# A macaron transformer block on one core: two mixer low parts made by accumulating transfers, a new order of the first matmuls of two norms, and the last sums, squares and output scalings in another order

## The chip, the cores and the metric

The kernel runs on one core of a Trainium2 chip. The metric is the device time of one execution in microseconds (us), median over the runs, lower is better. Before the change it is 996.78 us, the median of three runs (996.49, 996.78 and 1000.95).

TensorE multiplies, VectorE (DVE) and ScalarE (ACT) do the elementwise work, GpSimd (POOL) does a little of it and issues some transfers, and SyncE (SP) issues the others. Each engine works through its own instructions in their order and waits on semaphores for the others.

## The reference

One block over 512 tokens of width 1024, in float32. A vector `mod` of nine parts (shift, scale and gate for three sub-layers) comes from the condition `c`.

```python
u = modulate(rmsnorm(h, g_norm_ffn1[l]), sh1, sc1)
h = h + 0.5 * gt1 * swiglu(u, w_ffn1_in[l], w_ffn1_out[l])
u = modulate(rmsnorm(h, g_norm_mix[l]), sh2, sc2)
h = h + gt2 * token_mixing(u, ...)
u = modulate(rmsnorm(h, g_norm_ffn2[l]), sh3, sc3)
h = h + 0.5 * gt3 * swiglu(u, w_ffn2_in[l], w_ffn2_out[l])
...
return rmsnorm(h, g_final)
```

`swiglu` has 2816 hidden units. `token_mixing` projects `u` to pooling inputs, queries, keys, values and gates, and merges a pooling branch with a dilated attention.

## The kernel before, in words

**Layout.** Features lie on the partitions. `H[0..7]` hold h, 128 features by 512 tokens each. Most work near the norms is done in two halves of the tokens: A (called T1 in the output code) is tokens 0 to 255, B (T2) tokens 256 to 511.

**Precision.** Every product is made of three matmuls in a reduced 32-bit format: high part of the weight by high part of the activation, high by low, low by high (`mm3`, lines 363 to 365; the same three in `product` at 871 to 873 and in `plain` at 931 to 933). So each weight chunk of 128x1024 that a transfer brings to a `raw` buffer is split before use. `split_hi` has ACT copy it into the ring `whi` (L318), and `split_lo` has DVE subtract that from it into the ring `wlo` (L332). For chunks listed in `self.outer` the low part is made otherwise: ACT writes minus the high part into `wlo` (L314), and a transfer on POOL's queue adds the chunk from HBM onto it (L316), so that DVE has no part in it. Both rings have room for seven chunks. `fetch` issues the loads of the chunks on SP's queue (L241) when one of the three `raw` buffers comes free.

**The first feed-forward layer's last output part** runs in `out_quad` (seven products, i = 0 to 6, with sums of blocks, so that partial results are buffered in `kept`) and, for the last product, in `out_last`. There `to_h` adds a result to H (L877 from the buffers for H 4 to 7, L937 from a bank), `square` makes the squares for the next norm (ACT, L940), `add` sums them (DVE, L962), `stats_t` sums over the features by matmuls with ones (PE, L454), then ACT takes the root (L456), DVE the reciprocal (L459), and `spread` puts the result on all partitions by four matmuls (L464). `last(m)` is the end of one feature tile's second half. `more` splits weights ahead of need.

**The norm and the next layer's first matmuls.** `norm_steps` gives for each of eight feature tiles k three steps: DVE `ut` (L471), ACT the high part UH (L483), DVE the low part UL (L497). `head` (called for the mixer, n = 1, and for the second feed-forward layer, n = 2) starts the next layer while the norm is still being made: in half A for k = 0 to 3 the first three weight tiles (banks 0, 1, 2), then the fourth for the same k, then stats of half B, then k = 4 to 7 for all four, with the spread of half B between. The mixer's first four chunks are called base to base+3 here; base+3 is the fourth tile's.

**The end** (`out_last` with n = 2, then `out_end`). `scaled` multiplies H by the final gain into the output tile O (ACT, L944). Half A: ACT copies the spread norm into R (L572), POOL multiplies O 0 to 3 by it (`final_first`, L564), DVE multiplies O 4 to 7 by the bank itself (`final_second`, L564), SP stores. Half B: stats, root, reciprocal, spread (warm-up matmuls, L596, between), then the products of DVE and POOL and the stores.

**What sets the order.** Everything is written out by hand: the order of the calls in these functions is the order on every engine.

## Time and profile before

| | us |
|---|---|
| median of three runs | 996.78 |
| the profiled execution | 997.2 |
| its span, first to last instruction | 995.4 |
| TensorE busy, whole span | 980.2 |
| TensorE idle, 0 to 10 | 3.36 |
| TensorE idle, 10 to 320 | 0.27 |
| TensorE idle, 349 to 358 (head of the mixer) | 1.94 |
| TensorE idle, 400 to 480 | 0.47 |
| TensorE idle, 656.5 to 664 (head of the second feed-forward layer) | 0.14 |
| TensorE idle, 982.5 to 995.4 (the end) | 9.07 |
| VectorE / ScalarE / GpSimd busy | 828.1 / 565.1 / 70.8 |

The profiled execution was 0.4 us above the median. A row of the timeline gives start, length, engine, line, operation, tiles, count, and in brackets how long the engine was idle before it and whom it waited for. Lengths of neighbours overlap a little, so the cost of one among others is the distance of the starts.

### The profile page before, as it was taken

To read this page: it belongs to the slowest core of one execution; us is meant where nothing else is said; L and a number is where in the kernel's file an instruction comes from. 1 tells how busy PE (TensorE), PEld (TensorE's weight loads), DVE (VectorE), ACT (ScalarE), POOL (GpSimd) and SP (SyncE) were. 2 spreads that over 40 slices of the span, in tenths; PEclk is the share of its full clock that TensorE was granted. 3 is DMA by queue.
4 is the path that set the end of the run, shared out by engine and by line. 5 is a ranking of instruction groups with operands and counts; after the bars stand their busy time and mean duration, and the time that the engine had idled before them with its cause. 6 is when DMAs were issued, how large, how long until landed. Compare 5 with 4: busy or idle time off the path is not lost.

```text
span 995.4 us, 17274 instructions
## 1 busy us (share of the span) xinstructions
PE 980.2 (98%) x6962; PEld 916.0 (92%) x6962; DVE 828.1 (83%) x1260; ACT 565.1 (57%) x867; POOL 70.8 (7%) x80
## 2 busy tenths in 40 slices
PE   8999999999999999999999999999999999999996
PEld 6888899999999999889988888898999999999996
DVE  6979989999998877879667777578998989989875
ACT  6453286776768653233414323465677868676774
POOL 0000010110111000007100000000010110010001
PEclk9999999999999999999999999999999999999998
DMA  9867576877858422123364774223375566567522
GB/s 340 278 210 255 191 186 195 231 180 220 239 141 188 146 85 98 53 97 111 110 227 170 274 248 140 99 86 106 116 196 167 139 172 179 157 151 209 150 43 85
DMA packets 49746, 165.92 MB, mean 167 GB/s; under 512 B 5633, under 2 KB 8961, under 8 KB 49666
## 3 DMA queue, kind: packets, MB, share of 16 engines
q1 hardware_dynamic: 41778, 137.95, 39.5%
q0 software_dynamic: 7200, 26.22, 15.5%
q8 instruction: 54, 0.88, 0.3%
q10 hardware_dynamic: 688, 0.66, 0.2%
q14 instruction: 26, 0.21, 0.1%
HBM read 162.03 MB, written 2.77 MB: 166 GB/s over the span
## 4 chain that ended last, share of the span: by engine, by line
PE 92%; DVE 6%; issue 1%; ACT 1%; DMA 0%; DVEq 0%; ACTq 0%
PE bank L364 11%; PE bank L363 11%; PE bank L365 11%; PE bank L750 10%; PE bank L751 10%; PE bank L752 10%; PE bank L871 6%; PE bank L872 6%; PE bank L873 6%; PE bank L1751 1%; PE bank L1753 1%; PE bank L1755 1%; PE bank L1342 1%; DVE wlo L332 1%; DVE qz L1267 1%
## 5 line engine op out<-in xcount | busy, mean ns | idle before, releaser
L332 DVE TENSOR_TENSOR wlo<-raw,whi 128x1024 fp32r<-128x1024 f32 (+6 forms) x126 | 138.1, 1106 | 46.4 <-ACT whi L318 46.2
L363 PE MATMUL bank<-UH,whi 128*128 128x512 f32 (+1 forms) x432 | 158.1, 366 | 0.0
L364 PE MATMUL bank<-UL,whi 128*128 128x512 f32 (+1 forms) x432 | 154.2, 357 | 2.1 <-DVE UL L497 1.9
L318 ACT ACTIVATE whi<-raw 128x1024 fp32r<-128x1024 f32 (+5 forms) x157 | 149.1, 963 | 10.3 <-DMA raw<-wf1o 4.2
L365 PE MATMUL bank<-UH,wlo 128*128 128x512 f32 (+1 forms) x432 | 153.9, 356 | 0.0
L750 PE MATMUL bank<-UH,whi 128*128 128x256 f32 x512 | 141.4, 276 | 0.0
L752 PE MATMUL bank<-UH,wlo 128*128 128x256 f32 x512 | 141.4, 276 | 0.0
L751 PE MATMUL bank<-UL,whi 128*128 128x256 f32 x512 | 141.4, 276 | 0.0
L750 PE MATMUL bank<-SH,whi 128*128 128x256 f32 x384 | 107.0, 279 | 0.0
L752 PE MATMUL bank<-SH,wlo 128*128 128x256 f32 x384 | 106.9, 278 | 0.0
L751 PE MATMUL bank<-SL,whi 128*128 128x256 f32 x384 | 106.8, 278 | 0.0
L318 ACT ACTIVATE whi<-X 128x1024 fp32r<-128x1024 f32 (+2 forms) x98 | 91.9, 952 | 14.8 <-DVE X L257 14.7
L751 PEld LDWEIGHTS bank<-UL,whi 128*128 128x128 f32 x512 | 96.2, 188 | 0.1
L750 PEld LDWEIGHTS bank<-UH,whi 128*128 128x128 f32 x512 | 96.1, 188 | 0.1
L752 PEld LDWEIGHTS bank<-UH,wlo 128*128 128x128 f32 x512 | 96.1, 188 | 0.0
L364 PEld LDWEIGHTS bank<-UL,whi 128*128 128x128 f32 x432 | 81.2, 188 | 14.0 <-DVE UL L497 2.7
L332 DVE TENSOR_TENSOR wlo<-X,whi 128x1024 fp32r<-128x1024 f32 (+2 forms) x79 | 82.4, 1058 | 12.7 <-ACT whi L318 12.6
L365 PEld LDWEIGHTS bank<-UH,wlo 128*128 128x128 f32 x432 | 81.1, 188 | 12.1
L363 PEld LDWEIGHTS bank<-UH,whi 128*128 128x128 f32 x432 | 81.2, 188 | 11.4 <-issue 0.5
L871 PE MATMUL bank<-HI,whi 128*128 128x256 f32 x288 | 79.9, 277 | 0.0
L872 PE MATMUL bank<-HK,whi 128*128 128x256 f32 x288 | 79.5, 276 | 0.0
L873 PE MATMUL bank<-HI,wlo 128*128 128x256 f32 x288 | 79.5, 276 | 0.0
(349 smaller groups left out, 2456.0 us busy)
## 6 DMA issues: line engine op xcount, KB each, us to landing
ada<-wada SPq DMA_DIRECT2D x47, 512.0 KB, 5.3
raw<-wmix SPq DMA_DIRECT2D x44, 512.0 KB, 3.8
raw<-wf1i SPq DMA_DIRECT2D x33, 512.0 KB, 6.0
raw<-wf2i SPq DMA_DIRECT2D x31, 512.0 KB, 4.4
AR<-wada SPq DMA_DIRECT2D x16, 512.0 KB, 3.8
wlo<-wf2i POOLq DMA_DIRECT2D x16, 512.0 KB, 5.5
raw<-wf1o SPq DMA_DIRECT2D x15, 512.0 KB, 4.9
X<-wf2i SPq DMA_DIRECT2D x13, 512.0 KB, 7.1
```

The lines of the kernel that those rows point to most:

```text
L318: self.nc.scalar.activation(self.hi[:, y], r[:, x], AF.Copy)
L332: self.nc.vector.tensor_tensor(self.lo[:, y], r[:, x], self.hi[:, y], op=OP.subtract)
L363: M(ps, hi, uh, start=start, stop=False)
L364: M(ps, hi, ul, start=False, stop=False)
L365: M(ps, lo, uh, start=False, stop=stop)
L750: M(o, hi, uh, start=start and p == 0 and k == 0, stop=False, skip_group_check=True)
L751: M(o, hi, ul, start=False, stop=False, skip_group_check=True)
L752: M(o, lo, uh, start=False, stop=k == 3, skip_group_check=True)
L871: M(o, hi, uh, start=start and m % 2 == 0 and k == 0, stop=False, skip_group_check=True)
L872: M(o, hi, ul, start=False, stop=False, skip_group_check=True)
L873: M(o, lo, uh, start=False, stop=k == 1, skip_group_check=True)
L1267: self.nc.vector.tensor_scalar(qz[:, (2 * i + h) * P:(2 * i + h + 1) * P], q[:, toks], self.hmask[:, h:h + 1], None, op0=OP.mult)
```

## The change

- Four lines of `out_quad`: in the last output part H 4 to 7 get their buffered sums behind the copies of product 4, and no longer behind product 5.
- `plan`: base+2 and base+3 join `self.outer`. Their low parts are made by ACT and a transfer on POOL's queue.
- `head`: in half A for k = 0 to 3 the matmuls of the tiles in hand are grouped: all that take UH first, then those that take UL.
- `out_last` and `out_end`: `more` is called earlier a second time, with a limit of seven chunks from the part's start. In the second layer the scalings of half B leave their places behind each square, `final_second` is called twice, for O 4 and 5 ahead of `last(1)` and for O 6 and 7 behind the last sum, and three scalings stand behind the root.

```diff
+        self.outer.update({i: self.order[i][1] for i in (base + 2, base + 3)})
...
-    def final_second(self, rA):
+    def final_second(self, rA, m):
...
-        for j in range(4, KT):
+        for j in (m, m + 1):
             self.final(nc.vector, j, A, rA)
-            if j % 2:
-                self.store(j - 1, j + 1, A, nc.sync)
+        self.store(m, m + 2, A, nc.sync)
...
-        self.stats_t(rB, Bh, parts)
+        self.stats_t(rB, Bh, parts, between)
         warm(2)
-        nc.scalar.activation(self.O[3][:, Bh], self.H[3][:, Bh], AF.Copy, scale=self.g(3)[:, 3:4])
...
+                if h == 0 and i < 4:
+                    for x, y in ((0, 0), (1, 0), (0, 1)):
+                        for j in which:
+                            self.nc.tensor.matmul(banks[j][:, hs], w[j][k][x], (self.UH, self.UL)[y][k][:, hs],
+                                                  start=k == x == y == 0, stop=False)
+                    continue
...
                     copy(D[b][:, :, 1, :], r(A[b]))
-                elif i == 5 and tail:
-                    for m in (2 * b, 2 * b + 1):
+                    for m in (2 * b, 2 * b + 1) if tail else ():
                         to_h(4 + m, D[b][:, m % 2, :, :].rearrange("p h t -> p (h t)"), slice(0, T))
...
         def more():
-            if self.done < self.pos + 4:
+            if self.done < self.tail[n // 2] + 7:
...
-            if m < 3:
-                scaled(m, T2)
...
         pair(C, 0, T1, self.acc)
+        more()
         for m in (2, 3):
             plain(C, m, T1)
+        self.split_lo()
+        self.fetch()
...
-        if step:
+        if n:
+            self.final_second(rA, 4)
+            scaled(4, T2)
+            scaled(5, T2)
+        else:
             step(0)
-        for i in (4, 5, 6, 7):
-            scaled(i, T2)
-        more()
         last(1)
...
         sums.append(one(1))
+        scaled(6, T2)
...
-        self.split_lo()
-        self.fetch()
-        if n:
-            self.final_second(rA)
         last(3)
...
-        if not n:
+        if n:
+            self.final_second(rA, 6)
+            scaled(0, T2)
+            scaled(3, T2)
+        else:
             add(x, s)
+        self.fetch()
...
-            self.out_end(gate, (*self.late, s))
+            self.out_end((*self.late, s), lambda: [scaled(m, T2) for m in (1, 7, 2)])
```

**DVE, from the end of the first feed-forward layer into the mixer's norm.** H_72 to H_79 are H 0 to 7, AR holds the sums of squares, `sl` squares, raw_67 is the buffer of base+3. Before:

```order
L471 SCALAR_TENSOR_TENSOR ut<-H_74,mod,bank_104 128x256
L497 SCALAR_TENSOR_TENSOR UL<-ut,mod,UH 128x256
L937 SCALAR_TENSOR_TENSOR H_73<-bank_100,mod,H_73 128x256
L962 TENSOR_TENSOR AR<-AR,sl 128x256 x2
L332 TENSOR_TENSOR wlo<-raw_67,whi 128x1024
L471 SCALAR_TENSOR_TENSOR ut<-H_75,mod,bank_104 128x256
L497 SCALAR_TENSOR_TENSOR UL<-ut,mod,UH 128x256
L937 SCALAR_TENSOR_TENSOR H_75<-bank_101,mod,H_75 128x256
```

The same place after the change:

```order
L472 SCALAR_TENSOR_TENSOR ut<-H_74,mod,bank_104 128x256
L498 SCALAR_TENSOR_TENSOR UL<-ut,mod,UH 128x256
L941 SCALAR_TENSOR_TENSOR H_73<-bank_100,mod,H_73 128x256
L966 TENSOR_TENSOR AR<-AR,sl 128x256 x2
L472 SCALAR_TENSOR_TENSOR ut<-H_75,mod,bank_104 128x256
L498 SCALAR_TENSOR_TENSOR UL<-ut,mod,UH 128x256
L941 SCALAR_TENSOR_TENSOR H_75<-bank_101,mod,H_75 128x256
```

The subtraction of base+3's low part is gone from between the sums of squares and the fourth `ut`; the other steps stand as they stood. The one of base+2, some 25 rows earlier, is gone too, and there the four additions into H 4 to 7 now stand ahead of base+1's subtraction and no longer behind it. On ACT the two copies for each of base+2 and base+3 stand together ahead of squares of half A.

**PE, the first rows of the mixer's head.** bank_98, bank_99 and bank_102 are the first three weight tiles. Before:

```order
L363 MATMUL bank_98<-UH,whi 128x256
L364 MATMUL bank_98<-UL,whi 128x256
L365 MATMUL bank_98<-UH,wlo 128x256
L363 MATMUL bank_99<-UH,whi 128x256
L364 MATMUL bank_99<-UL,whi 128x256
L365 MATMUL bank_99<-UH,wlo 128x256
L363 MATMUL bank_102<-UH,whi 128x256
L364 MATMUL bank_102<-UL,whi 128x256
L365 MATMUL bank_102<-UH,wlo 128x256
```

After:

```order
L643 MATMUL bank_98<-UH,whi 128x256
L643 MATMUL bank_99<-UH,whi 128x256
L643 MATMUL bank_102<-UH,whi 128x256
L643 MATMUL bank_98<-UH,wlo 128x256
L643 MATMUL bank_99<-UH,wlo 128x256
L643 MATMUL bank_102<-UH,wlo 128x256
L643 MATMUL bank_98<-UL,whi 128x256
L643 MATMUL bank_99<-UL,whi 128x256
L643 MATMUL bank_102<-UL,whi 128x256
```

The first matmul that takes UL was the second of nine and is now the seventh. The head of the second feed-forward layer changes likewise.

**DVE at the end of the program.** `u` holds the late sums of squares, bank_98 the spread norm of half A. Before:

```order
L937 SCALAR_TENSOR_TENSOR H_74<-bank_100,mod,H_74 128x256
L937 SCALAR_TENSOR_TENSOR H_73<-bank_103,mod,H_73 128x256
L962 TENSOR_TENSOR u_9435<-u_9435,sl 128x256 x2
L564 TENSOR_TENSOR out<-out,bank_98 128x256 x4
L937 SCALAR_TENSOR_TENSOR H_75<-bank_100,mod,H_75 128x256
L962 TENSOR_TENSOR u_9435<-u_9435,sl 128x256
L459 RECIPROCAL r_90<-r_90 128x2
```

After:

```order
L941 SCALAR_TENSOR_TENSOR H_74<-bank_100,mod,H_74 128x256
L565 TENSOR_TENSOR out<-out,bank_98 128x256 x2
L941 SCALAR_TENSOR_TENSOR H_73<-bank_103,mod,H_73 128x256
L966 TENSOR_TENSOR u_9437<-u_9437,sl 128x256 x2
L941 SCALAR_TENSOR_TENSOR H_75<-bank_100,mod,H_75 128x256
L966 TENSOR_TENSOR u_9437<-u_9437,sl 128x256
L565 TENSOR_TENSOR out<-out,bank_98 128x256 x2
L460 RECIPROCAL r_90<-r_90 128x2
```

Two of the four output products now stand ahead of H 1's addition, two behind the last sum of squares.

More of the change, by code (lines that the diff above doesn't have):

```diff
@@ L576, in final_first, with out_end @@
                 self.store(j - 1, j + 1, A, nc.sync)
-    def final_second(self, rA):
+    def final_second(self, rA, m):
         nc, A = self.nc, slice(0, HT)
-        for j in range(4, KT):
+        for j in (m, m + 1):
             self.final(nc.vector, j, A, rA)
-            if j % 2:
-                self.store(j - 1, j + 1, A, nc.sync)
-    def out_end(self, gate, parts):
+        self.store(m, m + 2, A, nc.sync)
+    def out_end(self, parts, between):
         nc = self.nc
@@ L901, in out_quad @@
                     copy(D[b][:, :, 1, :], r(A[b]))
-                elif i == 5 and tail:
-                    for m in (2 * b, 2 * b + 1):
+                    for m in (2 * b, 2 * b + 1) if tail else ():
                         to_h(4 + m, D[b][:, m % 2, :, :].rearrange("p h t -> p (h t)"), slice(0, T))
-                elif i == 5:
+                elif i == 5 and not tail:
                     v.tensor_tensor(D[b][:, :, 0, :], r(B[b]), D[b][:, :, 0, :], op=OP.add)
```

## The prediction

> **What bounds the kernel now.** The page gives busy time over the span:
>
> ```profile
> PE 980.2 (98%) x6962; PEld 916.0 (92%) x6962; DVE 828.1 (83%) x1260; ACT 565.1 (57%) x867; POOL 70.8 (7%) x80
> ```
>
> PE is the bound, so what counts is where its 15 us of idle time lie. I read the same by stretches next. Columns: the stretch, its length, then busy time and instruction count of PE, its weight loads, DVE, ACT and POOL, then the granted clock, the DMA share and GB/s.
>
> ```profile
> 349.00:358.00 9.00, 7.06 (x59) 6.67 (x58) 8.20 (x20) 5.14 (x11) 0.00 (x0) 1.00 0.28 97
> 656.50:664.00 7.50, 7.36 (x61) 6.96 (x60) 6.51 (x18) 6.39 (x14) 0.00 (x0) 1.00 0.17 63
> 760.00:976.00 216.00, 216.00 (x1898) 216.00 (x1897) 187.36 (x233) 157.44 (x222) 18.28 (x21) 1.00 0.58 150
> 982.50:995.40 12.90, 3.83 (x30) 3.26 (x28) 4.87 (x14) 2.58 (x8) 2.50 (x4) 0.73 0.49 163
> ```
>
> PE has no gap in the long stretches (216.00 of 216.00 us, 1898 matmuls, 0.114 each). Work removed from DVE or ACT there is worth nothing. The change's two places are where PE does wait: the mixer's head, where it is idle 1.94 us of 9.00 while DVE is busy 8.20, and the end. PE's own waits name whom it waits for:
>
> ```profile
> PE bank L364 <- DVE UL L497: 1.9, 2, 1.1
> PE bank L454 <- DVE u L962: 1.5, 1, 1.5
> ```
>
> The first row is the mixer's head (two waits for low parts of u), the second the last sum of squares. Together they are 3.4 us of 995, so no outcome of this change that fills them reaches 0.5% (5.0 us), which is about what a measurement of this kernel can tell from no change.
>
> **Sums into H sooner, and the squares of the first layer's output.** DVE's rows, ACT's two, PE's one:
>
> ```profile
> 334.19 2.74 DVE L877 SCALAR_TENSOR_TENSOR H<-kept,mod,H 128x512 f32<-128x512 f32 x4
> 336.84 1.22 DVE L332 TENSOR_TENSOR wlo<-raw,whi 128x1024 fp32r<-128x1024 f32 x1
> 341.71 1.49 DVE L962 TENSOR_TENSOR AR<-AR,sl 128x512 f32<-128x512 f32 x2
> 331.96 2.00 ACT L318 ACTIVATE whi<-raw 128x1024 fp32r<-128x1024 f32 x2
> 338.49 0.81 ACT L940 ACTIVATE AR<-H 128x256 f32<-128x256 f32 x2 [4.52 <-DVE H L937]
> 343.51 0.94 PE L454 MATMUL bank<-ones,AR 128*128 128x1 f32 x8
> ```
>
> Moving the four additions (2.74) forward and dropping base+2's subtraction lets DVE reach H 0 about two to three us sooner. But the last sum ends at 341.71 + 1.49 = 343.20, and PE reaches the matmuls that read it at 343.51 without a wait: PE's own work hides all of it, so its price is nothing. The freed time pays for what ACT gets: two more copies of 1.0 us each (two took 2.00) and base+3's high part moved here, three in all, two of them between the first and the later squares. ACT had idled 4.52 before the squares, so the three fit and the last sum should not come later than today. Were that cover gone, each us would cost one. Queued behind the new ACT copies are those squares, behind them DVE's sums, behind those PE's statistics. The POOL queue gets two issues and nothing of its own stands behind them until the pooling some 100 us later; on SP the buffers of base+2 and base+3 come free from ACT and no longer from DVE, so the loads of base+5 and base+6 start sooner and nothing waits for them.
>
> **Two low parts by transfers: the mixer's head.** DVE's rows, then PE's:
>
> ```profile
> 348.87 0.48 DVE L497 SCALAR_TENSOR_TENSOR UL<-ut,mod,UH 128x256 fp32r<-128x256 f32 x1
> 350.32 1.22 DVE L332 TENSOR_TENSOR wlo<-raw,whi 128x1024 fp32r<-128x1024 f32 x1
> 351.46 0.48 DVE L471 SCALAR_TENSOR_TENSOR ut<-H,mod,bank 128x256 f32<-128x256 f32 x1
> 351.85 0.48 DVE L497 SCALAR_TENSOR_TENSOR UL<-ut,mod,UH 128x256 fp32r<-128x256 f32 x1
> 354.01 0.48 DVE L497 SCALAR_TENSOR_TENSOR UL<-ut,mod,UH 128x256 fp32r<-128x256 f32 x1
> 357.43 0.16 DVE L459 RECIPROCAL r<-r 128x2 f32<-128x2 f32 x1
> 351.04 0.28 PE L363 MATMUL bank<-UH,whi 128*128 128x256 f32 x1
> 352.39 0.38 PE L364 MATMUL bank<-UL,whi 128*128 128x256 f32 x1 [1.08 <-DVE UL L497]
> 354.54 0.38 PE L364 MATMUL bank<-UL,whi 128*128 128x256 f32 x1 [0.86 <-DVE UL L497]
> 355.59 0.95 PE L454 MATMUL bank<-ones,AR 128*128 128x1 f32 x8
> 357.90 0.61 PE L464 MATMUL bank<-cst,r 128*128 128x128 f32 x4
> ```
>
> The subtraction at 350.32 (base+3) stands in DVE's way between the third and fourth `ut`: 351.46 - 350.32 = 1.14 us by start to start. Without it the low parts of k = 2 and 3 end at 351.19 and 353.35 in place of 352.33 and 354.49. DVE goes on back to back from there, so the reciprocal of half B ends at 357.59 - 1.14 = 356.45.
>
> PE, with the UH matmuls first at 0.114 each: k = 2 starts at 351.04 as before, its six UH matmuls last to 351.72, and UL is there. Three more to 352.06, six of k = 3 to 352.74, then it waits for UL until 353.40 (0.05 behind its end, as before). The remaining three take 0.4 (eight took 355.59 - 354.54 = 1.05), statistics start at 353.8, and from there to the spread it is 357.90 - 355.59 = 2.31, so PE is at the spread at 356.1. But the spread reads the reciprocal of 356.45, so it starts at 356.50: **1.40 us sooner**. Grouping UH alone adds about 0.1 of that, since the reciprocal decides. Bounds: 1.14, if the spread keeps its old distance to the reciprocal, and 1.8, if PE's arrival decided. I take 1.40, because the row of the reciprocal is what the spread has to wait for.
>
> The two transfers must be in time. Landing of all 50 transfers of this kind (the row of the line that issues them, us):
>
> ```profile
> DMA to landing us min/median/max: 5.0/5.6/9.4
> ```
>
> ACT has written minus base+2's high part one copy behind base+1's, at 331.96 + 2.0 = about 333.9, and base+3's behind the first two squares, by 338.49 + 0.81 + 1.0 = 340.3 at the latest. The head starts 18 matmuls before 351.04, at 349.0; PE reads base+2's low part from the sixth on, 349.6, and base+3's from 353.8. So 15.7 and 13.5 us are there for 9.4 at most.
>
> [...]
>
> After 358 PE has almost no gaps and DVE's further steps hang on PE's banks, so I carry the whole 1.40 to the end.
>
> **High parts first in the second feed-forward layer's head.** PE's first wait and its spread, and DVE's reciprocal:
>
> ```profile
> 657.01 0.38 PE L364 MATMUL bank<-UL,whi 128*128 128x256 f32 x1
> 663.21 0.71 PE L464 MATMUL bank<-cst,r 128*128 128x128 f32 x4
> 662.99 0.16 DVE L459 RECIPROCAL r<-r 128x2 f32<-128x2 f32 x1
> ```
>
> PE no longer stalls at 657.01, but the spread at 663.21 already starts 0.06 behind the reciprocal's end (663.15), and DVE's chain to it is not touched. What PE wins early it waits at the spread: 0, with 0.1 at most either way.
>
> **The end.** DVE's rows, then POOL's, PE's, ACT's two, and the lengths of the late sums:
>
> ```profile
> 981.13 0.48 DVE L937 SCALAR_TENSOR_TENSOR H<-bank,mod,H 128x256 f32<-128x256 f32 x1 [0.73 <-PE bank L933]
> 981.54 1.45 DVE L962 TENSOR_TENSOR u<-u,sl 128x256 f32<-128x256 f32 x2
> 982.91 1.40 DVE L564 TENSOR_TENSOR out<-out,bank 128x256 f32<-128x256 f32 x4
> 984.24 0.47 DVE L937 SCALAR_TENSOR_TENSOR H<-bank,mod,H 128x256 f32<-128x256 f32 x1
> 984.63 0.41 DVE L962 TENSOR_TENSOR u<-u,sl 128x256 f32<-128x256 f32 x1
> 986.92 0.17 DVE L459 RECIPROCAL r<-r 128x2 f32<-128x2 f32 x1 [1.89 <-ACT r L456]
> 980.39 3.19 POOL L564 TENSOR_TENSOR out<-out,AR 128x256 f32<-128x256 f32 x4 [24.99 <-ACT AR L572]
> 985.10 0.61 PE L454 MATMUL bank<-ones,u 128*128 128x1 f32 x4 [1.52 <-DVE u L962]
> 980.82 2.10 ACT L944 ACTIVATE out<-H,vecs 128x256 f32<-128x256 f32 x5
> 988.35 0.38 ACT L606 ACTIVATE AR<-bank 128x256 f32<-128x256 f32 x1 [1.06 <-DVE out L564]
> L962 DVE TENSOR_TENSOR u<-u,sl x4: 409/634/954, 979.3 to 984.6; 128x256 f32<-128x256 f32 x3, 128x512 f32<-128x512 f32 x1
> ```
>
> The four output products (1.40, 0.35 each) stand between the sums and H 3's addition, on the path to PE's wait of 1.52. In the change two of them (0.70) fit into DVE's wait of 0.73 for PE before 981.13, and two stand behind the last sum, where DVE idles 1.89. So H 3's addition starts at 982.91 in place of 984.24, 1.33 us sooner, and its square on ACT with it. The last sum then starts at 983.30, while POOL still runs its products (980.39 to 983.58). Of the late sums the one in the clear took 0.409 and the longest, at POOL's side, 0.954: beside POOL it may cost up to 0.54 more. POOL will start some 0.1 to 0.2 sooner, since ACT no longer has a scaling (0.42) ahead of R, so only 0.1 of the overlap is left. I take **1.2**; bounds 0.8 (the whole 0.54) and 1.5 (POOL's earlier start freeing the first sum too).
>
> [...]
>
> On ACT three scalings stand behind the root where one stood. Five took 2.10, so two more cost 0.84, and ACT idles 1.06 there for DVE's first product: hidden, 0.1 late at most.
>
> **Sum.** 1.40 + 0 + 1.2 = 2.6. The profiled execution took 997.2, 995.4 of span and 1.8 around it, and would take 994.6. It stands 0.4 above the median of 996.78, so I forecast 994.2.
>
> **Rivals.**
>
> *The mixer's gain is given back.* Behind the head some DVE stretch, or a chunk's load, becomes the last to end, and PE only waits elsewhere. For it: DVE is over 80% busy over the span. Against: PE has no gap in the long stretches, and the list of its waits names no transfer. The end alone then gives 996.78 - 1.2 = 995.6.
>
> *The end's gain is lost to POOL and ACT.* The last sum takes the whole 0.54 and R comes 0.2 late: 996.78 - 1.4 - 0.6 = 994.8. For it is the 0.954 row.
>
> *The second head's gain stays.* If the reciprocal were not what the spread waits for, 0.4 more: 993.8. The reciprocal's row speaks against it.
>
> *Slower: the accumulating transfers come late.* Place: base+2's low part, read from 349.6. Nothing is lost until it lands 15.7 us after ACT's copy at 333.9; each us beyond is PE idle. To undo the 2.6 it would have to land at 352.2, 18.3 us after, about twice the longest of the 50. Then the time is 997 and above.
>
> **How the numbers follow.** Forecast 0.68, mixer's gain given back 0.14, end lost 0.10, second head 0.04, slower 0.04. The range takes both gains at their upper bounds and 0.1 for the second head (3.4, so 993.4) and 0.4 for the spread of runs, hence 993.0, and above the first rival with the end at its lower bound 0.8 (996.0) and the same 0.4, 996.4. Faster by over 0.5% needs 991.8, more than all the waits in reach, 0.02; slower by over 0.5% only in a part of the last rival, 0.02; the rest, 0.96, is within 0.5%.
>
> **What would show it.** In the profile after: in the mixer's head one short wait for UL (about 0.6) at k = 3 and a new one at the spread for the reciprocal; the spread 1.4 sooner after the head's start. In the second head no wait for UL but one of about 0.4 at the spread. At the end PE's wait for the last sum down from 1.52 to about 0.3, and a last sum longer than 0.409. Statistics of half A in the first layer without a wait. I am wrong if PE waits at the mixer's head for `wlo`, if it waits at 343.5 for the sums, or if its stretches between 358 and 976 show new gaps.

## The result and the profile after

| | before | after |
|---|---|---|
| median of 22 runs each, us | 998.08 | 994.70 |
| lowest to highest, us | 996.49 to 1005.30 | 993.96 to 998.76 |
| the profiled execution, us | 997.20 | 995.64 |

The ratio of after to before is 0.9958, with a 95% interval of 0.9942 to 0.9973. The forecast was 994.2 from 996.78, a ratio of 0.9974: just outside that interval, on the small side. The time itself, 994.7, is 0.5 from the forecast, and the ratio stands for no change by the 0.5% bound, though its interval reaches past it.

The run times lie in groups. Of before's 22, 13 are between 996.5 and 998.4 (median 997.20) and 9 between 1000.9 and 1005.3; of after's, 16 are between 994.0 and 995.6 (median 994.48) and 6 between 997.0 and 998.8. The lower groups differ by 2.72 us, close to the forecast's 2.6. The rest of the ratio comes from the upper groups, and a later run shows where before's begin.

The page of after, its row of busy times: PE is busy 1.1 us more than before, DVE 2.2 us less.

```profile
PE 981.3 (99%) x6962; PEld 916.8 (92%) x6962; DVE 825.9 (83%) x1258; ACT 567.2 (57%) x869; POOL 72.4 (7%) x82
```

The same three places by stretches, columns as before (PE, its weight loads, DVE, ACT, POOL, granted clock, DMA share, GB/s):

```profile
349.00:358.00 9.00, 8.29 (x70) 7.89 (x69) 7.80 (x21) 5.32 (x10) 0.00 (x0) 1.00 0.14 38
656.50:664.00 7.50, 7.02 (x61) 6.81 (x60) 6.51 (x18) 5.94 (x14) 0.00 (x0) 1.00 0.11 45
982.50:993.80 11.30, 4.05 (x30) 3.37 (x28) 4.21 (x12) 3.05 (x8) 2.35 (x4) 0.66 0.55 186
```

In the mixer's head PE is idle 0.71 of 9.00 us where it was idle 1.94. The second head shows more idle time than before, 0.48 against 0.14. The list of PE's waits names them:

```profile
PE bank L465 <- DVE r L460: 0.7, 2, 0.5
PE bank L643 <- DVE UL L498: 0.5, 1, 0.5
PE bank L455 <- DVE u L966: 0.2, 1, 0.2
```

The two waits for UL (1.9) became one of 0.5, the wait at the end went from 1.5 to 0.2, and there is a new kind: 0.7 in two waits of the spread for the reciprocal, one in each head. No row names `wlo` or the sums in AR. PE's rows at the four places (start, length, engine, line, tiles, count, in brackets the idle time before and whom it waited for):

```profile
343.88 0.95 PE L455 MATMUL bank<-ones,AR 128*128 128x1 f32 x8
...
349.36 0.50 PE L643 MATMUL bank<-UH,whi 128*128 128x256 f32 x3
...
353.77 0.63 PE L643 MATMUL bank<-UL,whi 128*128 128x256 f32 x3 [0.51 <-DVE UL L498]
354.24 0.95 PE L455 MATMUL bank<-ones,AR 128*128 128x1 f32 x8
356.88 0.71 PE L465 MATMUL bank<-cst,r 128*128 128x128 f32 x4 [0.21 <-DVE r L460]
...
662.55 0.71 PE L465 MATMUL bank<-cst,r 128*128 128x128 f32 x4 [0.48 <-DVE r L460]
...
983.77 0.61 PE L455 MATMUL bank<-ones,u 128*128 128x1 f32 x4 [0.23 <-DVE u L966]
```

From half A's statistics to half B's spread of the mixer's norm are 356.88 - 343.88 = 13.00 us; before they were 357.90 - 343.51 = 14.39. DVE's rows beside them:

```profile
341.18 1.48 DVE L966 TENSOR_TENSOR AR<-AR,sl 128x512 f32<-128x512 f32 x2
...
350.69 0.47 DVE L472 SCALAR_TENSOR_TENSOR ut<-H,mod,bank 128x256 f32<-128x256 f32 x1
...
356.66 0.16 DVE L460 RECIPROCAL r<-r 128x2 f32<-128x2 f32 x1
...
980.28 0.74 DVE L565 TENSOR_TENSOR out<-out,bank 128x256 f32<-128x256 f32 x2
...
982.77 0.47 DVE L941 SCALAR_TENSOR_TENSOR H<-bank,mod,H 128x256 f32<-128x256 f32 x1
983.16 0.55 DVE L966 TENSOR_TENSOR u<-u,sl 128x256 f32<-128x256 f32 x1
983.64 0.74 DVE L565 TENSOR_TENSOR out<-out,bank 128x256 f32<-128x256 f32 x2
```

The sums of half A end at 342.66, 1.2 us ahead of PE (0.31 before). The `ut` at 350.69 now stands directly behind DVE's sums of squares, with no subtraction between. The reciprocal's end, 356.82, decides the spread. At the end two output products stand ahead of H 1's addition and two behind the last sum.

### The profile page after: what moved, and what is told of

The parts are those of the page before. It is cut to its first block, busy times and chain, and to the rows that moved or that the text cites. A ratio compares the mean times of both kernels' runs of the same rounds, so it can differ in the third digit from the quotient of the medians.

```text
span 993.8 us, 17278 instructions
## 1 busy us (share of the span) xinstructions
PE 981.3 (99%) x6962; PEld 916.8 (92%) x6962; DVE 825.9 (83%) x1258; ACT 567.2 (57%) x869; POOL 72.4 (7%) x82
## 4 chain that ended last, share of the span: by engine, by line
PE 92%; DVE 6%; issue 1%; ACT 1%; DMA 1%; SPq 0%; DVEq 0%; ACTq 0%
PE bank L364 10%; PE bank L756 10%; PE bank L366 10%; PE bank L365 10%; PE bank L755 10%; PE bank L757 10%; PE bank L877 6%; PE bank L876 6%; PE bank L878 6%; PE bank L1759 1%; PE bank L1763 1%; PE bank L1761 1%; PE bank L1350 1%; DVE wlo L333 1%; DVE qz L1275 1%
## 5 line engine op out<-in xcount | busy, mean ns | idle before, releaser
L333 DVE TENSOR_TENSOR wlo<-raw,whi 128x1024 fp32r<-128x1024 f32 (+6 forms) x124 | 135.6, 1103 | 44.5 <-ACT whi L319 44.3
L364 PE MATMUL bank<-UH,whi 128*128 128x512 f32 (+1 forms) x408 | 151.6, 372 | 0.0
L366 PE MATMUL bank<-UH,wlo 128*128 128x512 f32 (+1 forms) x408 | 147.5, 362 | 0.0
L365 PE MATMUL bank<-UL,whi 128*128 128x512 f32 (+1 forms) x408 | 147.3, 361 | 0.0
L756 PEld LDWEIGHTS bank<-UL,whi 128*128 128x128 f32 x512 | 96.2, 188 | 0.1
L755 PEld LDWEIGHTS bank<-UH,whi 128*128 128x128 f32 x512 | 96.1, 188 | 0.1
L757 PEld LDWEIGHTS bank<-UH,wlo 128*128 128x128 f32 x512 | 96.1, 188 | 0.0
L366 PEld LDWEIGHTS bank<-UH,wlo 128*128 128x128 f32 x408 | 76.8, 188 | 12.1
L365 PEld LDWEIGHTS bank<-UL,whi 128*128 128x128 f32 x408 | 76.7, 188 | 11.4 <-issue 0.5
L364 PEld LDWEIGHTS bank<-UH,whi 128*128 128x128 f32 x408 | 76.7, 188 | 11.3 <-issue 0.5
```

Source lines behind the costliest of these rows:

```text
L333: self.nc.vector.tensor_tensor(self.lo[:, y], r[:, x], self.hi[:, y], op=OP.subtract)
L364: M(ps, hi, uh, start=start, stop=False)
L365: M(ps, hi, ul, start=False, stop=False)
L366: M(ps, lo, uh, start=False, stop=stop)
L755: M(o, hi, uh, start=start and p == 0 and k == 0, stop=False, skip_group_check=True)
L756: M(o, hi, ul, start=False, stop=False, skip_group_check=True)
```

## The experiments

The theory of the prediction: the mixer's head is quicker because transfers take base+3's subtraction off DVE, and the end because H 3's addition comes sooner. Its rival: the transfers have no part in it, and the subtraction only had to go elsewhere. Since the run times lie in groups, I compare the stages inside the traces, each from one landmark row of PE to another. "Head" is half A's statistics to half B's spread; "to second head" is the mixer's spread of half A to the same spread of the next norm; "second layer" goes from there to the same spread at the end; "end" is half A's statistics there to half B's first row that reads `u`. The ends of matmuls in these rows are modelled, and a bracket shows only the idle time behind such an end, so a wait of 0.1 or 0.2 us shows in the distance of two starts alone.

| kernel | head | to second head | second layer | end | median us |
|---|---|---|---|---|---|
| before | 14.39 | 307.89 | 325.41 | 8.29 | 998.08 |
| after | 13.00 | 306.87 | 326.03 | 6.99 | 994.70 |
| e1, no transfers | 13.11 | 306.85 | 325.40 | 7.00 | 995.41 |
| e2, late split | 16.04 | 310.34 | 325.40 | 6.99 | 998.10 |
| e3, no high part first | 13.23 | 307.20 | 325.40 | 6.98 | 994.59 |
| e4, spread later | 13.98 | 306.24 | 324.70 | 6.98 | 993.35 |
| e5, early split only | 13.57 | 307.02 | 325.41 | 8.28 | 1000.21 |
| e6, sums late | 13.10 | 306.90 | 325.41 | 6.99 | 994.12 |
| e7, old end | 12.99 | 307.05 | 325.41 | 8.28 | 995.55 |
| e8, no transfers, spread and copy moved | 14.17 | 306.14 | 324.70 | 6.99 | 993.75 |
| e9, spread and copy moved | 14.06 | 306.10 | 324.70 | 7.00 | 993.10 |
| e10, before again | 16.90 | 311.31 | 325.41 | 8.27 | 1001.52 (one run) |
| e11, before again | 14.37 | 308.51 | 325.41 | 8.28 | 997.56 (one run) |
| e12, after again | 12.99 | 306.67 | 325.40 | 7.00 | 994.60 (one run) |

In e4, e8 and e9 half B's spread stands a step later, so their "head" isn't comparable.

**e1: without the transfers.** Base+2 and base+3 get their low parts on DVE again, at the early place.

```diff
-        self.outer.update({i: self.order[i][1] for i in (base + 2, base + 3)})
```

> The changed kernel, but base+2 and base+3 are split as before (ACT high part, DVE subtraction) and keep their new early place. Theory (the mixer's head gains because DVE is freed of two subtractions, which only the transfers can do): DVE has the 2 x 1.14 us again, now between 334 and 341 where it has under 2 us free; the last sum of half A comes about 0.6 to 1.0 late, PE waits that long at the statistics near 343.9, and about 0.7 of the head's 1.4 us is lost. Rival (moving base+3's split out of DVE's dense stretch is enough, the transfers are for nothing): no wait at the statistics, head from its start to its spread as short as in the changed kernel (7.5 us; before 8.9), time within 0.2 us of the changed kernel.

Measured: 995.41 us (994.25 to 998.00), ratio 0.9956 (0.9936 to 0.9976), by the run times the same as the full change. DVE's rows, then PE's:

```profile
332.98 2.35 DVE L332 TENSOR_TENSOR wlo<-raw,whi 128x1024 fp32r<-128x1024 f32 x2
...
337.55 1.23 DVE L332 TENSOR_TENSOR wlo<-raw,whi 128x1024 fp32r<-128x1024 f32 x1 [1.43 <-ACT whi L318]
...
341.65 1.48 DVE L965 TENSOR_TENSOR AR<-AR,sl 128x512 f32<-128x512 f32 x2
```

```profile
342.81 0.28 PE L936 MATMUL bank<-HX,wlo 128*128 128x256 f32 x1
343.18 1.05 PE L454 MATMUL bank<-ones,AR 128*128 128x1 f32 x8
...
353.18 0.62 PE L642 MATMUL bank<-UL,whi 128*128 128x256 f32 x3 [0.51 <-DVE UL L497]
...
356.29 0.71 PE L464 MATMUL bank<-cst,r 128*128 128x128 f32 x4 [0.18 <-DVE r L459]
```

Base+3's subtraction stands at 337.55, behind a wait of DVE for ACT of 1.43 us, and the sums end at 343.13. PE's last matmul ahead of the statistics starts at 342.81. In after the statistics follow 0.12 behind that matmul (343.76 and 343.88); here they follow 0.37 behind it, just behind the sums, so they are 0.25 late. The head is 13.11 us, and from that last matmul to the spread are 13.48 us, against 13.12 in after and 14.51 before. So most of it is the rival's: 1.03 of the 1.39 us come without the transfers, from splitting base+3 early and, for 0.1 to 0.2, from the grouping (e3). The transfers are worth the other 0.36, about half of what the theory gave them.

**e2: the transfers, but the second split at its late place.** The call of `more` goes back to its old place ahead of `last(1)`, with its old limit; base+3's part then is copied and sent there.

```diff
-        more()
         for m in (2, 3):
...
+        more()
         last(1)
```

> The changed kernel, but the second call that splits ahead stands in its old late place, so base+3's two copies on ACT and its transfer come between the high parts of u of the mixer's norm. Theory (the transfer needs the early place): ACT writes minus the high part near 349.5, the transfer lands some 5.6 us later near 355, while PE wants base+3's low part near 354; PE waits for wlo 1 to 2 us and for the third high part of u up to 1 us, and most of the head's 1.4 us is gone (head from start to spread 8.5 to 10 us against 7.5). Rival (the place does not matter): head 7.5 us, no wait for wlo.

Measured: 998.10 us (996.32 to 1000.92), ratio 0.9991 (0.9971 to 1.0010): the whole gain is gone. PE's row, and the transfer's issue to landing in the groups of its line:

```profile
357.17 0.58 PE L366 MATMUL bank<-UH,wlo 128*128 128x256 f32 x1 [2.04 <-DMA wlo<-wmix]
```

```profile
DMA to landing us min/median/max: 7.4/7.4/7.4
```

The transfer is issued at 349.7 and lands 7.4 us after, so PE stands 2.04 us. That explains two thirds of the 3.04 by which the head is longer (16.04 against 13.00). The rest lies behind the wait, where PE's starts are 0.213 apart until 360, for 0.114 otherwise; e10 comes back to it. DVE has no subtraction of base+3 here either, so a free DVE isn't enough: the low part has to be there when PE reads it.

**e3: without the high parts first**, the grouping in `head` taken out.

```diff
-                if h == 0 and i < 4:
...
-                    continue
```

> The changed kernel, but both heads take the matmuls of one tile together again (UH high, UL high, UH low), as before. Theory (the spread's reciprocal decides, so grouping is worth about 0.1 us in the mixer's head and nothing in the second layer's): mixer's head from start to spread 7.6 us, second head 6.7 us as in the changed kernel, waits for UL back at both and no wait at the second spread. Rival (grouping is worth its own waits): mixer's head about 8.2 us, second head 7.1 us.

Measured: 994.59 us (993.87 to 997.04), ratio 0.9955 (0.9938 to 0.9973). PE's rows:

```profile
353.67 0.39 PE L365 MATMUL bank<-UL,whi 128*128 128x256 f32 x1 [0.85 <-DVE UL L498]
354.71 0.95 PE L455 MATMUL bank<-ones,AR 128*128 128x1 f32 x8
...
357.01 0.61 PE L465 MATMUL bank<-cst,r 128*128 128x128 f32 x4
```

PE waits once, for 0.85, and comes to the spread when the reciprocal is there. The grouping is worth 13.23 - 13.00 = 0.23 in the mixer's head, and 0.13 at the matmul behind the spread (at 357.37 here and 357.34 in after), since the spread behind its wait took 0.10 longer (0.71 against 0.61). The run times can't tell so little. In the second head, statistics to spread are 12.09 here, 12.06 in after, 12.08 before: worth nothing, because the spread there starts 0.05 to 0.07 behind the reciprocal's end either way.

**e4: half B's spread one product step later**, in both heads, to see whether the new waits for the reciprocal cost anything.

```diff
-                    if i == 8:
+                    if i == 9:
                         self.spread(self.B[7], Bh)
-                    if i > 7:
-                        stepB(i - 8)
+                    if i > 8:
+                        stepB(i - 9)
```

> The changed kernel, but in both heads the spread of half B and the norm steps behind it stand one k later (12 matmuls more before it). Theory (PE's waits at the two spreads, 0.21 and 0.48 us, are waits for the reciprocal alone, and the grouped order's gain in the second head lies hidden there): both waits go, about 0.7 us less in all, 0.2 before the mixer's body and 0.5 before the second layer's. Rival (the norm of half B then comes late and PE waits for its UL or UH in half B): the same or up to 1 us slower.

Measured: 993.35 us (992.59 to 995.68), ratio 0.9942 (0.9918 to 0.9965). In the list of PE's waits, after's row of 0.7 for the reciprocal is gone; what is left of the three places is the wait for UL and the one at the end:

```profile
PE bank L643 <- DVE UL L498: 0.5, 1, 0.5
PE bank L455 <- DVE u L966: 0.2, 1, 0.2
```

The stretch to the second head is 306.24, and the second layer 324.70 against 325.40: 0.4 to 0.6 (against e12 and after) and 0.7 us less. So the waits did cost. Each gain is more than the wait it removed (0.21 and 0.48); where the rest comes from isn't shown. The run's interval overlaps after's.

**e5: the early split alone**, on the kernel before: no transfers, the sums into H where they were, the old end.

```diff
-            if self.done < self.pos + 4:
+            if self.done < self.tail[n // 2] + 7:
...
+        more()
         for m in (2, 3):
```

> The kernel before with one edit: base+3 is split at the early place of the changed kernel, by ACT and DVE, no transfers, sums into H at their old place, old orders elsewhere. Theory (the early place gives the head's gain, and the sooner sums are the cover that pays for it): DVE now has base+3's 1.14 us and a wait for its high part between the first H additions, half A's last sum of squares ends near 345.8 in place of 343.2, and PE waits 2 to 2.5 us at the statistics of half A; the head after it is 1.1 to 1.3 us shorter (statistics of half A to spread of half B, 14.4 before, near 13.2), net about 1 us slower. Rival (the sooner sums are worth nothing, as the prediction had it): no wait at the statistics, 1.2 us faster.

Measured: 1000.21 us (998.35 to 1002.66), ratio 1.0009 (0.9993 to 1.0026). DVE's rows, then PE's:

```profile
343.19 1.23 DVE L332 TENSOR_TENSOR wlo<-raw,whi 128x1024 fp32r<-128x1024 f32 x1 [1.44 <-ACT whi L318]
...
347.29 1.48 DVE L962 TENSOR_TENSOR AR<-AR,sl 128x512 f32<-128x512 f32 x2
```

```profile
348.82 1.05 PE L454 MATMUL bank<-ones,AR 128*128 128x1 f32 x8 [2.24 <-DVE AR L962]
```

Now the subtraction's wait for ACT is on the path, and PE stands 2.24 us for the sums. Without that wait PE would have been there at 346.58, so this execution is also 3.07 us late from earlier on (below). From 346.58 to the spread of the second head at 658.35 are 311.77 us, against 310.19 before (343.51 to 653.70): 1.6 us slower, though the head behind the wait is shorter. The lowest run is 1.5 above before's lowest of that set (996.88). So the early split has to be paid for ahead of 343 us. A part of the loss is PE's granted clock, 0.52 from 351 to 353 us, behind the wait (see e10).

**e6: the sums into H back behind product 5**, everything else as changed.

```diff
-                    for m in (2 * b, 2 * b + 1) if tail else ():
+                elif i == 5 and tail:
+                    for m in (2 * b, 2 * b + 1):
```

> The changed kernel, with the buffered sums into H 4 to 7 back behind product 5. Theory (the transfers free as much of DVE as the sooner sums do, either covers the other): half A's last sum ends near 343.3, PE waits 0 to 0.2 us at the statistics, time within 0.2 us of the changed kernel, statistics of half A to spread of half B 13.0 us as there. Rival (the sums on time are what the early split needs in any case): a wait of 1 us or more at the statistics.

Measured: 994.12 us (994.00 to 994.53), ratio 0.9957 (0.9940 to 0.9974). PE's row:

```profile
343.15 1.05 PE L455 MATMUL bank<-ones,AR 128*128 128x1 f32 x8
```

The matmul ahead of it starts at 342.91, so the statistics are 0.12 late. With the transfers the earlier sums are hardly needed; without the transfers (e1) they are what pays, but for 0.25. Either of the two is nearly enough, the change has both, and with neither (e5) PE waits 2.24.

**e7: the old end**, everything else as changed.

```diff
-        if n:
-            self.final_second(rA, 4)
-            scaled(4, T2)
-            scaled(5, T2)
...
+        if n:
+            self.final_second(rA, 4)
+            self.final_second(rA, 6)
         last(3)
```

> The changed kernel with the end's edits undone: the scalings behind each square, the four output products of DVE together behind the two sums, one scaling behind the last root. Theory: PE's wait for the last sum is back at 1.5 us; from the statistics of half A to those of half B 8.29 us as before, against 6.99 in the changed kernel, so 1.3 us slower than that. Rival (PE's matmuls or the stores set the end anyway): 7.0 to 7.3 us, and the same time as the changed kernel.

Measured: 995.55 us (994.60 to 999.11), ratio 0.9966 (0.9945 to 0.9987). PE's row at the end:

```profile
983.74 0.61 PE L455 MATMUL bank<-ones,u 128*128 128x1 f32 x4 [1.52 <-DVE u L966]
```

The wait of 1.52 is back to the digit, and the end's stage is 8.28 against 6.99. The new end is worth 1.29 us by itself and the rest doesn't lean on it.

**e8 and e9: the spread later, and a copy of v ahead of a product that waits for its weights.** Near 500 us part of the lead was lost, in after from 1.01 us at 481 to 0.66 at 502. DVE's rows there, of after:

```profile
498.15 1.23 DVE L387 SCALAR_TENSOR_TENSOR AR<-AR,cond 128x1024 f32<-128x1024 f32 x1 [3.34 <-DMA AR<-wada]
...
499.31 0.69 DVE L1539 COPY v<-bank 128x512 f32<-128x512 f32 x1
```

The copy that PE needs next stands behind a product whose weights come 3.34 us after DVE is free, 3.12 in before. PE had a lead of 1.01 us at 481, this product starts only 0.44 sooner than in before (498.15 against 498.59). Both runs put the copy first; e8 also drops the transfers.

```diff
-                    if k == 6 or (k == 2 and c == 3):
+                    if (k == 6 and c < 3) or (k == 2 and c == 3):
                         self.bg()
                 v.tensor_copy(self.v23[:, c, :], b)
+                if c == 3:
+                    self.bg()
```

> The changed kernel without the two transfers, with the spread of half B one k later in both heads (as in the run above where that stood alone), and with the mixer's last value copy on DVE ahead of the condition product that waits for its weights (both before the gates). Theory (PE waits 0.3 us near 500 because DVE's copy stands behind a product that waits 3 us for a transfer whose pace does not move with PE): that wait goes too, and the time is 0.3 us under the run with the later spread, near 993.0. Rival (the wait moves to the next product or the split behind it): as that run, near 993.4, or slower.

> The changed kernel with its transfers, with both heads' second spread one product step later, and with the last copy of v ahead of the bias product that waits for its weights near 500 us. If the 0.16 us that the kernel with the later spreads lost on PE between 480 and 503 us (its lead over the kernel before went from 1.29 to 1.13) hangs on that copy, the lead keeps its value there, and the run is 0.1 to 0.3 us below the 993.35 us of the later spreads alone: about 993.1 us. If the copy is only one of several things that hold the place, the lead still shrinks and the time is that of the later spreads, 993.3 us. With the transfers the statistics of the mixer head's half A show no wait of PE (0.38 us without them in the combination tried before).

Measured: e8 993.75 us (992.74 to 996.20), ratio 0.9951 (0.9934 to 0.9968); e9 993.10 us (992.03 to 995.84), ratio 0.9938 (0.9914 to 0.9962). DVE's row of e9:

```profile
499.20 0.69 DVE L1539 COPY v<-bank 128x512 f32<-128x512 f32 x1 [2.51 <-PE bank L1533]
```

The copy now waits for PE alone, and e9's distance to before doesn't change between 471 and 657. That part was right, and e9 is the quickest kernel of the study, though its interval overlaps those of e4 and after. e8 keeps its distance there too. Its median is 0.65 above e9's, which their intervals don't tell apart, but its list of PE's waits has a row that e9's lacks:

```profile
PE bank L454 <- DVE AR L965: 0.4, 1, 0.4
```

Without the transfers DVE's sums come late at 343: by 0.25 in e1, and here by 0.54 (the last matmul ahead of the statistics starts at 344.06, the statistics at 344.72). So the transfers do buy something: a quarter of the head's gain, and, with the earlier sums, 1.2 us of slack for an execution in which DVE runs a little behind.

**e10, e11, e12: before twice and after once**, both unchanged, to see where the groups of run times part.

> The kernel before, once more, for its start. The runs of the kernel before lie in two groups, near 997 and from 1001 to 1005 us, those of the changed kernel near 994.5 and 997 to 999. If the start is what divides them, a run of the upper group has PE 3 us or more behind at 17 us from the span's start, as the profile of the early split alone had (2.85 us), and runs level with the lower group from there; a run of the lower group is within 0.7 us of the first profile there. If the division comes later, the offset at 17 us is under 0.7 us in both and grows at one place further on.

> The kernel before, a third look, for the same question: near 997 us with an offset under 0.7 us at 17 us, or 1001 us and more with 3 us there (the start divides the groups), or 1001 us and more with a small offset there and a step at a later place (it does not).

> The changed kernel, once more, for its start and for the 0.62 us that its first profile lost in the second layer between 664 and 680 us (326.03 us from the second head's first spread to that of the end, against 325.41 before). If that loss belongs to that execution, this one shows 325.4 us there; if it belongs to the changed kernel, 326.0 again. Time 994.2 to 994.7 us, or near 997 us with an offset of 3 us at 17 us.

Measured: 1001.52, 997.56 and 994.60 us. e10 fell into before's upper group, and the start was not the cause: PE is 0.25 us behind at 17 us, and so it stays until 355. By stretches, before's first profile and then e10:

```profile
356.00:362.00 6.00, 6.00 (x54) 6.00 (x55) 3.82 (x9) 4.01 (x7) 0.00 (x0) 1.00 0.01 2
```

```profile
356.00:362.00 6.00, 6.00 (x30) 6.00 (x30) 1.99 (x6) 2.47 (x4) 0.00 (x0) 0.51 0.06 21
```

In the same 6 us PE gets through 30 matmuls where it got through 54, at a granted clock of 0.51. It begins right behind the second of the two waits for UL:

```profile
352.60 0.38 PE L364 MATMUL bank<-UL,whi 128*128 128x256 f32 x1 [1.07 <-DVE UL L497]
...
354.75 0.39 PE L364 MATMUL bank<-UL,whi 128*128 128x256 f32 x1 [0.84 <-DVE UL L497]
...
355.29 0.42 PE L364 MATMUL bank<-UL,whi 128*128 128x256 f32 x1
355.51 0.41 PE L365 MATMUL bank<-UH,wlo 128*128 128x256 f32 x1
```

The stretch to the second head is 311.31 against 307.89, 3.4 us more, and the two later stages are as in the first profile. So in e10 the waits of before came with more than their length: 1.9 us, and some 3 more at a granted clock of 0.51 behind them.

Put beside the other profiles, this makes an order for this place. Behind one wait of over 2 us the clock fell both times (e2, whose granted clock is 0.50 from 358 to 360 us, and e5, 0.52 from 351 to 353). Behind before's two waits of 1.9 in sum it fell in one profile of three. Where the single waits are 0.85 or less and half as long in sum (after, e1, e3, e4, e6 to e9, e12) it fell in none of nine.

Why in one of three? In the traces of before, after and e10 the entries of the granted clock stand whole multiples of 3.413 us apart, from the first to the last: in before at 12.29 and 988.50, 286 steps; in after at 9.93, 13.35, 16.76 and 986.14, also 286 from first to last; in e10 at 13.76, 17.17, 355.09 and 361.92, where 355.09 is 100 steps behind 13.76. Where this grid lies differs from execution to execution. In e10 both waits fall between two of its points, all but 0.15 us; in before's first profile there is a point between them. Before's first profile, then e10, cut at the grid:

```profile
350.21:353.62 3.41, 2.33 (x19) 2.00 (x17) 3.20 (x8) 0.93 (x2) 0.00 (x0) 1.00 0.25 82
353.62:357.04 3.42, 2.56 (x22) 2.50 (x22) 3.24 (x10) 2.08 (x5) 0.00 (x0) 1.00 0.48 173
```

```profile
351.68:355.09 3.41, 1.65 (x11) 1.45 (x12) 3.20 (x10) 1.43 (x3) 0.00 (x0) 1.00 0.54 157
355.09:358.50 3.41, 3.41 (x19) 3.41 (x18) 2.56 (x7) 1.91 (x5) 0.00 (x0) 0.50 0.34 93
```

PE was busy 1.65 us of a step ahead of the fall in e10, and 1.46 in e2; in before's first profile it was busy 2.33 and 2.56, in e11 2.34 and 2.57, and the clock stayed. So in these three executions the clock fell where the same two waits lay in one step, and stayed where two steps shared them. Busy time is not the whole measure: in e5 it was 2.27 ahead of the fall, with eight matmuls of one column among the 19, and near the start the clock fell for one step in after, e4, e8, e10 and e12, in after from 13.35 to 16.76 (0.50), with no wait over 0.2 us but with 16 matmuls of one column among the 29 of the step ahead. What decides it isn't shown.

The run times agree. Of the 71 runs of before that were taken beside the experiments, 25 took over 1000.9 us, and 22 of these have a mean granted clock of 0.989 to 0.993 (e10: 0.990), against 0.995 to 0.997 in the 38 runs below 998.6. All of after's 22 have 0.994 or more, and its upper group 0.996 and 0.997. So nearly all of before's upper group lost clock and none of after's did; at which place is shown for e10 alone.

The start is what moves e5 and e9: before's first profile and e5 from 12 to 20 us.

```profile
12.00:20.00 8.00, 7.73 (x51) 6.81 (x52) 7.15 (x19) 4.19 (x7) 0.00 (x0) 1.00 1.04 404
```

```profile
12.00:20.00 8.00, 8.00 (x39) 8.00 (x39) 4.31 (x15) 2.79 (x6) 0.00 (x0) 1.00 1.03 398
```

PE does 39 matmuls for 51, and e9 and e5 are 2.7 and 2.9 us behind at 17 us, which no line of their edits touches. The clock's column says 1.00 in both rows, but it has nothing to read there: e5's trace has its first entry of the clock, the change to full, at 19.99 us, e9's at 19.50, and before's first profile at 12.29. Such a start would put an execution of after at 997 to 998, where its upper group lies; e9's profile (995.20) is from the upper of its own two groups (992.0 to 993.1 and 995.2 to 995.8). No run of after's upper group was profiled, so for after this is inferred. e12 shows 325.40 for the second layer: the 0.62 us that after's first profile lost there belonged to that execution (from 664 to 680 PE did 36 matmuls in 4 us for 38, without a gap; why isn't shown). e11 lost 0.6 near 500 against before's first profile, so the loss there is the kernel before's too.

## Why the prediction was right, and where it was not

**Where the time is lost.** Right: what the change filled are PE's waits at these two places. What came with such waits beyond their length, some 3 us in e10, is missing (see the sum).

**Sums into H sooner, priced at nothing.** Nearly right in the sum: with the old place (e6) the statistics are 0.12 late and the head is 13.10 for 13.00. The prediction's reason, cover by PE's work, is half of it: DVE's room ahead of 343 is where the early split of base+3 is paid, and the sums or the transfers make that room. The cover is 0.31 us before and 1.2 with both; with one of the two it is gone and PE starts 0.12 (e6) or 0.25 (e1) late.

**The mixer's head, 1.40.** The size was right: 14.39 - 13.00 = 1.39, with all three signs (UL wait 0.51 for 0.6 expected, a wait at the spread, 0.21 for 0.4, the reciprocal deciding). The chain was right too: base+3's subtraction left the place between the third and fourth `ut`, and the reciprocal came sooner. The step that failed is the credit, "Two low parts by transfers": e1 has 1.03 of the 1.39 without them, and e2 has them, and DVE free, without the gain. What counts is that base+3's low part is made early, by DVE or by a transfer. The prediction mentions the earlier place only as a load on ACT. The grouping's 0.1 was 0.23 at the spread's start and 0.13 behind it (e3).

The transfers were in time. Their issue and landing in after, from the groups of their line:

```profile
L317 POOL DMA_DIRECT2D wlo<-wmix x2: 862/864/865, 334.7 to 338.6; - x2
DMA to landing us min/median/max: 7.4/8.4/9.3
```

Issued at 334.7 and 338.6 and landed within 9.3, they are there by 347.9, 1.5 us ahead of the head's start at 349.36.

**Carried whole to the end.** Open by some tenths: against the first profile of before the stretch to the second head gained 1.02 in after and 1.22 in e12, of 1.39; against e11 it gained 1.64 and 1.84. The difference arises near 500, at a transfer that DVE waits for: against before's first profile after lost 0.34 there, e12 0.16 and e11 0.60, while e8 and e9, with the copy of v first, lost nothing. The rival "The mixer's gain is given back" looked for a transfer in PE's list of waits, which names only DVE's copy of v (0.2); the transfer is in DVE's list.

**High parts first in the second head, 0.** Right, mechanism and all: no wait for UL and 0.48 at the spread in after, and the same stretch without the grouping (e3).

**The end, 1.2.** Right: 8.29 - 6.99 = 1.30 in after and 1.29 in e7. H 3's addition came 1.44 us sooner, measured from half A's spread (984.24 - 979.11 and 982.77 - 979.08), for 1.33 expected. The last sum took 0.55 for 0.41, 0.14 longer, not 0.54. POOL's row:

```profile
980.25 3.19 POOL L565 TENSOR_TENSOR out<-out,AR 128x256 f32<-128x256 f32 x4 [24.87 <-ACT AR L573]
```

POOL's last product ends at 983.44, 0.20 behind the addition's end at 983.24. The last sum starts at 983.16, so 0.28 us of it lie beside that product; in before it starts at 984.63, 1.05 behind the end of POOL's (983.58), and takes the 0.41. So a sum with POOL still at work was longer here too, but why by 0.14, and by 0.54 in before, isn't shown. The three scalings behind the root stayed hidden: ACT's copy of R starts 1.44 behind the spread where it was 1.21, but this spread took 0.96 us for 0.71 and the copy only waited for DVE's product.

**The sum, 2.6.** 2.72 between the lower groups. What the prediction lacked is a term: it priced before's waits at their length, 3.4 us in all, and took that as a bound, while in e10 PE's granted clock was 0.51 behind the same waits, at some 3 us more. By means, the two sets of 22 differ by 999.62 - 995.40 = 4.2 us and the lower groups by 997.32 - 994.64 = 2.7, so some 1.5 us of the difference lies in how often and how far runs fall into the upper groups. The slower rival, transfers late, shows its mechanism in e2, a wait of PE for `wlo`, though with base+3's low part and not base+2's, and because its copy was started late. In after nothing waits for them.

## What to carry to other kernels

A gain has to be tested against each part of an edit apart: here the part that looked like the cause (the transfers) carried a quarter of the head's gain, and the earlier place of one split most of the rest, with two nearly interchangeable ways to pay for it. A wait of the bounding engine may come with more than its length (1.9 us of waits and some 3 us behind them in e10), so removing one can be worth more than the profile of a quick execution says; look at the spread of the run times before pricing it. And a lead won early can go at a step in line behind a transfer (in after 0.34 us of 1.0, near 500), which was found in the waits of the engine that feeds the bound; the bound's own list named only that engine.

## What the runs showed of the hardware

- **TensorE's granted clock changed at whole multiples of 3.413 us**, from the first entry of a trace to its last (976.21 us, 286 steps, in before and in after; 100 steps from 13.76 to 355.09 in e10). At a granted clock of 0.50 matmul starts were 0.213 apart for 0.114 (e2, e10). That clock lasted one step in e2 and e5 and two in e10. It fell when one step held most of PE's idle time (busy 1.65 of 3.41 us in e10, 1.46 in e2), and stayed when the same waits were shared by two steps (2.33 and 2.56 in before, 2.34 and 2.57 in e11).
- **The first entry of the granted clock came at another time in each execution.** It is at 9.93 us in after's first profile, at 12.29 in before's and at 19.99 in e5, whose PE ran 39 matmuls for 51 from 12 to 20 us; ahead of its first entry the clock's column says 1.00 and means nothing.
- **The accumulating transfers of 512 KB took 7.4 and 9.3 us from issue to landing** in after's mixer stretch, at the long end of what before's 50 took (5.0 to 9.4).
